# A two-layer decoder trunk: the products of the gate and up pairs and of the down pairs issued in source order

## The chip, the core and the metric

The kernel runs on one core of a Trainium2 chip. The metric is the device time of one launch in microseconds (us). The time before is the median of three runs.

## What is computed

The reference is a trunk of two layers for one sequence of 256 tokens and a width of 2048, all in float32. A layer has a mixing half (attention heads and a gated recurrence that share one input and one output projection), a feed-forward half, and a gated embedding at its end. Each half is normed before and after it:

```python
for i in range(DEPTH):                      # DEPTH = 2
    h = rms_norm(x, pre_mix_gain[i])
    m = hybrid_mixer(h, positions, w_in[i], ..., w_out[i])
    x = x + rms_norm(m, post_mix_gain[i])
    h = rms_norm(x, pre_ffn_gain[i])
    f = (jax.nn.silu(h @ w_ffn_gate[i]) * (h @ w_ffn_up[i])) @ w_ffn_down[i]
    x = x + rms_norm(f, post_ffn_gain[i])
    gate = jax.nn.sigmoid(rms_norm(x, ple_gain[i]) @ w_ple_gate[i])
    x = x + (p[i] @ w_ple_proj[i]) * gate
```

The three matrices of the feed-forward half are 2048 x 5632 (gate, up) and 5632 x 2048 (down). The change lies in their multiplications.

## The kernel before

**Products.** Tokens stand on the 128 partitions in two tiles, t = 0 and 1. A weight is read in chunks of 256 x 512 (`fetch_w`, two halves k of 128 rows). Each chunk is split into a high part `wh`, a cast by ScalarE (line 305), and a low part `wl`, a subtraction by VectorE (line 315); the activations are split likewise into `xh` and `xl` (lines 203 and 204, into tiles named `ck`). A product of one half of a chunk with one token tile is then three matmuls of 128 x 128 by 128 x 512 into one PSUM bank: xh by wh (line 431), xl by wh (line 434) and xh by wl (line 435). A chunk with one token tile is thus six matmuls. `strip` (lines 330 to 333) multiplies one column strip of a weight in this way.

**Pairs.** `paired` multiplies two column strips together, wa into the banks e and a (token tiles 0 and 1), wb into the banks c and d, where d is the bank u again. For most chunks it does so plainly (`plain`): wa over all other chunks, then wb over them. For one pair of chunks (q and q + 1, and a half of q + 2 in the gate and up pairs) it takes seven block products in the place of eight: sums and differences of the activations' four blocks (`mix(1)` to `mix(4)`, tiles named `sum` or `nat`) meet sums and differences of the weights' chunks, which VectorE makes in place in the raw chunks (`sub`, line 447). The order in the source is this. `fast()` makes u (a bank of the tag `ms`), which ScalarE copies out (`saved(u)`, line 440), then c, which is copied too, then e, then a. `plain` then takes the first of the other chunks with wa into e and a, and behind it `second()` is called: it adds the product of `mix(2)` onto u, nine matmuls with `sum` operands in a gate and up pair, six with `nat` operands in a down pair, and copies u out again. In a gate and up pair, and in most down pairs, `plain` then goes on with the rest of wa, and `third()` follows it: `mix(4)` onto c, `mix(3)` onto u, a third copy of u. With `mixed_order` (the first down pair of a group of three) the last two chunks of the group are left until `third()` and the other chunks of wb have been done, since the group's last hidden strip is then still on its way.

**What runs over what.** In the feed-forward half of a layer the 5632 hidden columns are 11 strips of 512, n = 0 to 10. Strip 0 is done by `strip`, strips 1 to 10 each by a gate and up pair (`gated`). They are taken in groups of 2, 3, 3 and 3 (`FF_GROUPS`); with the first group one strip more is made ahead. After each group come its down products: the four output strips as two pairs, or, in the last group, one pair and two single strips. A layer has so 10 gate and up pairs and 7 down pairs. `paired` also does the two pairs of the output projection `w_out` and one pair of the gated embedding at the layer's end (with `after`). A finished hidden strip goes through VectorE and DRAM (`shuffled`: a store and four fetches, line 264, into `nat` tiles), and `split_shuffled` splits its token tiles a few chunks later (`later`, `tick`).

**What sets the order.** ScalarE, VectorE and TensorE each carry out their own instructions in order and wait for each other by semaphores. The source is recorded first, and a scheduler then decides in which order the instructions of each engine stand; it may put one ahead of another of the source where data allow it. `tc.high_priority` and `behind(name)` (place after the instruction last marked by that name; "pe" is the last product) are used here and there to steer it. The buffers of weights are `wps` (7 of `wh`, 7 of `wl`) and `wpr` (10 raw chunks): a cast into a `wh` buffer waits until TensorE has finished with what was in it. PSUM has four banks `acc` (c, e, a among them) and four banks `ms` (u).

## Time and profile before

| | |
|---|---|
| median of the runs | 2397.57 us |
| lowest and highest | 2392.6 and 2398.31 us |
| the profiled execution's own time | 2398.53 us |
| its span, first to last instruction | 2396.7 us |
| mean granted clock of TensorE | 0.995 |
| TensorE busy (PE) | 2365.4 us, 99% of the span |
| VectorE busy (DVE) | 1997.5 us, 83% |
| ScalarE busy (ACT) | 1401.3 us, 58% |
| DMA engines, bytes moved | 506.04 MB, 211 GB/s over the span |

The profile is of one execution. PE is TensorE's matmuls, PEld its weight loads, DVE VectorE, ACT ScalarE, SP the engine that issues most DMAs. A row of the timeline has the start in us, the length, the engine, the line of the kernel, the operation, the tile written and the tile read by the program's names, their shapes, and in square brackets how long the engine was idle before and what ended that. Matmuls overlap: one starts 0.23 us behind another in a dense stretch and is shown 0.39 long. In the list of waits a row has the waiting engine, tile and line, then what released it, and then the total in us, the number of times and the longest.

### The profile page before, as it was taken

The page shows a single profiled execution, that of the slowest core. Times are in us where ns is not written, and L with a number is a line of the kernel's source. Part 1 is how long each engine was busy: PE and PEld are TensorE (multiplying, and loading weights), DVE is VectorE, ACT ScalarE, POOL GpSimd, SP SyncE. Part 2 cuts the span into 40 slices and gives each one's busy share as a digit, 9 for nine tenths or more (in the row PEclk, how much of TensorE's full clock was granted, in tenths as well). Part 3 has the DMA queues.
Part 4 walks back from the last instruction along what each step waited for, and adds up shares of the span by engine and source line. Part 5 has one row for each costly group of instructions (what it writes and reads, how often), then busy time and mean ns, then how long its engine had stood idle before and what let it go on. Part 6 is the DMA issues. An engine that isn't in the chain of part 4 may idle for free. (4 is left out here: it accounts for less than half of the span.)

```text
span 2396.7 us, 31644 instructions
## 1 busy us (share of the span) xinstructions
PE 2365.4 (99%) x10951; PEld 1955.7 (82%) x10951; DVE 1997.5 (83%) x2647; ACT 1401.3 (58%) x2000; POOL 104.3 (4%) x213
## 2 busy tenths in 40 slices
PE   9999999999999999999999999999999999999999
PEld 7888887878878878878788888878787888788787
DVE  7687987999988889887867879789898989888785
ACT  6555466566555655656656554565566565565564
POOL 3100001000000000001010000010000000000010
PEclk9999999999999999999999999999999999999999
DMA  8666467666557665765776563675667575666753
GB/s 290 213 193 198 145 211 252 205 226 231 194 198 236 214 228 180 270 213 189 233 224 211 174 223 129 226 255 176 228 211 230 195 256 185 205 220 237 242 166 132
DMA packets 301665, 506.04 MB, mean 211 GB/s; under 512 B 23712, under 2 KB 69696, under 8 KB 301504
## 3 DMA queue, kind: packets, MB, share of 16 engines
q1 hardware_dynamic: 301200, 503.93, 63.5%
q8 instruction: 86, 1.41, 0.2%
q14 instruction: 75, 0.61, 0.1%
q10 hardware_dynamic: 240, 0.07, 0.0%
q0 software_dynamic: 64, 0.02, 0.0%
HBM read 474.57 MB, written 29.36 MB: 210 GB/s over the span
## 5 line engine op out<-in xcount | busy, mean ns | idle before, releaser
L305 ACT CAST wh<-wr 128x1024 fp32r<-128x1024 f32 x980 | 1012.1, 1052 | 794.9 <-DVE wr L447 215.4
L315 DVE TENSOR_TENSOR wl<-wr,wh 128x1024 fp32r<-128x1024 f32 x980 | 1169.2, 1220 | 252.8 <-ACT wh L305 233.7
L330 PE MATMUL acc<-wh,ck 128*128 128x512 f32 x1056 | 417.8, 396 | 0.8 <-ACT ck L203 0.8
L331 PE MATMUL acc<-wh,ck 128*128 128x512 f32 x1056 | 413.5, 392 | 0.0
L333 PE MATMUL acc<-wl,ck 128*128 128x512 f32 x1056 | 411.9, 391 | 0.8 <-DVE wl L315 0.8
L447 DVE TENSOR_TENSOR wr<-wr 128x1024 f32<-128x1024 f32 (+1 forms) x240 | 243.4, 1042 | 1.2
L333 PEld LDWEIGHTS acc<-wl,ck 128*128 128x128 f32 x1056 | 198.5, 188 | 42.9 <-DVE wl L315 1.7
L331 PEld LDWEIGHTS acc<-wh,ck 128*128 128x128 f32 x1056 | 199.0, 188 | 40.2 <-DVE ck L204 0.4
L330 PEld LDWEIGHTS acc<-wh,ck 128*128 128x128 f32 x1056 | 198.5, 188 | 40.7 <-ACT ck L203 1.0
L431 PE MATMUL acce<-wh,ck 128*128 128x512 f32 x468 | 183.1, 391 | 8.6 <-ACT ck L203 8.6
L434 PE MATMUL acce<-wh,ck 128*128 128x512 f32 x468 | 183.6, 392 | 3.3 <-DVE ck L204 3.3
L431 PE MATMUL acca<-wh,ck 128*128 128x512 f32 x468 | 182.2, 389 | 0.6 <-ACT nat L1285 0.6
L435 PE MATMUL acce<-wl,ck 128*128 128x512 f32 x468 | 182.2, 389 | 0.0
L435 PE MATMUL acca<-wl,ck 128*128 128x512 f32 x468 | 182.1, 389 | 0.0
L434 PE MATMUL acca<-wh,ck 128*128 128x512 f32 x468 | 182.1, 389 | 0.0
L435 PE MATMUL ms<-wl,ck 128*128 128x512 f32 x440 | 171.5, 390 | 4.0 <-DVE wl L315 4.0
L431 PE MATMUL ms<-wh,ck 128*128 128x512 f32 x440 | 172.5, 392 | 0.0
L434 PE MATMUL ms<-wh,ck 128*128 128x512 f32 x440 | 171.3, 389 | 0.0
L434 PE MATMUL accc<-wh,ck 128*128 128x512 f32 x368 | 143.2, 389 | 0.0
L435 PE MATMUL accc<-wl,ck 128*128 128x512 f32 x368 | 143.2, 389 | 0.0
L431 PE MATMUL accc<-wh,ck 128*128 128x512 f32 x368 | 143.2, 389 | 0.0
L431 PEld LDWEIGHTS acce<-wh,ck 128*128 128x128 f32 x468 | 87.8, 188 | 28.8 <-ACT ck L203 11.1
(285 smaller groups left out, 3252.1 us busy)
## 6 DMA issues: line engine op xcount, KB each, us to landing
wr<-in_w_in_dram SPq DMA_DIRECT2D x176, 512.0 KB, 4.7
wr<-in_w_ffn_gate_dram SPq DMA_DIRECT2D x176, 512.0 KB, 5.2
wr<-in_w_ffn_up_dram SPq DMA_DIRECT2D x176, 512.0 KB, 6.0
wr<-in_w_ffn_down_dram SPq DMA_DIRECT2D x176, 512.0 KB, 6.9
wr<-in_w_out_dram SPq DMA_DIRECT2D x64, 512.0 KB, 4.6
wr<-in_w_ple_gate_dram SPq DMA_DIRECT2D x64, 512.0 KB, 5.0
turn<-nat SPq DMA_DIRECT2D x86, 256.0 KB, 2.6
nat<-turn SPq DMA_DIRECT2D x344, 64.0 KB, 3.5
```

The lines of the kernel that those rows point to most:

```text
L305: marks["hi"] = S.copy(hi, raw)
L315: marks["lo"] = V.tensor_tensor(lo, raw, hi.bitcast(F32), op=ALU.subtract)
L330: T.matmul(ps[t], xh, hi[:, k], start=first, stop=False)
L331: T.matmul(ps[t], xl, hi[:, k], start=False, stop=False)
L333: marks[t, c] = marks["pe"] = T.matmul(ps[t], xh, lo[:, k], start=False, stop=last)
L431: T.matmul(ps, xh, hi[:, k], start=id(ps) not in opened, stop=False, skip_group_check=True)
L434: T.matmul(ps, xl, hi[:, k], start=False, stop=False, skip_group_check=True)
L435: marks["pe"] = T.matmul(ps, xh, lo[:, k], start=False, stop=k == ks[-1], skip_group_check=True)
L447: V.tensor_tensor(dst, p, q, op=ALU.subtract)
```

## The change

`paired` gets an argument `free`. Its body after `fast()` becomes an inner function `products`, and for every pair that is neither `free` nor has `after` that body is recorded in a manual schedule for TensorE: TensorE's instructions keep the order in which the source issues them. `fast()` is placed behind the product issued last before it. The two `w_out` pairs are passed `free=True`, so they and the pair of the gated embedding are recorded as before. The order of the other engines is still the scheduler's.

```diff
@@ -410,7 +410,7 @@
         return both
 
     def paired(lhs, sums, wa, wb, cols, done_a, done_b, nch=8, row0=0, skews=(0, 0),
-               after=None, mixed_order=False, half=None, q=0):
+               after=None, mixed_order=False, half=None, q=0, free=False):
 
         base = row0 // (2 * P)
         opened = {}
@@ -529,30 +529,37 @@
             if end:
                 end(1)
 
-        e, a, c, d, x1, x2, second, third = fast()
-
-        def end_a(t):
-            done_a(t, (e, a)[t], x1[t])
-
-        def end_b(t):
-            done_b(t, (c, d)[t], x2[t])
-        if mixed_order:
-            plain(wa, cols[0], (e, a), 0, None, cs=rest[:-2], then=second)
+
+        def products(pin):
+            with behind("pe") if pin else nullcontext():
+                e, a, c, d, x1, x2, second, third = fast()
+
+            def end_a(t):
+                done_a(t, (e, a)[t], x1[t])
+
+            def end_b(t):
+                done_b(t, (c, d)[t], x2[t])
+            if mixed_order:
+                plain(wa, cols[0], (e, a), 0, None, cs=rest[:-2], then=second)
+                third()
+                plain(wb, cols[1], (c, d), 0, None, cs=rest[:-2])
+                plain(wa, cols[0], (e, a), 0, end_a, cs=rest[-2:])
+                plain(wb, cols[1], (c, d), 0, end_b, cs=rest[-2:])
+                return
+            def then():
+                second()
+                if after:
+                    after[0]()
+            plain(wa, cols[0], (e, a), skews[0], lambda t: t or end_a(t), then=then)
             third()
-            plain(wb, cols[1], (c, d), 0, None, cs=rest[:-2])
-            plain(wa, cols[0], (e, a), 0, end_a, cs=rest[-2:])
-            plain(wb, cols[1], (c, d), 0, end_b, cs=rest[-2:])
-            return
-        def then():
-            second()
+            end_a(1)
             if after:
-                after[0]()
-        plain(wa, cols[0], (e, a), skews[0], lambda t: t or end_a(t), then=then)
-        third()
-        end_a(1)
-        if after:
-            after[1]()
-        plain(wb, cols[1], (c, d), skews[1], end_b)
+                after[1]()
+            plain(wb, cols[1], (c, d), skews[1], end_b)
+
+        pin = not (after or free)
+        with tc.manual_schedule(engines={T.engine}) if pin else nullcontext():
+            products(pin)
 
     def load_gain(g, col):
         b = np_.tile([P, W], F32, tag="gB", name="gB", bufs=2)
@@ -1174,7 +1181,7 @@
             return summed(done)
         for s in (0, 2):
             paired(mixT, lambda: sums, w_out[l], w_out[l], (s * W, s * W + W), merged(s),
-                   merged(s + 1), skews=(0, SKEW if s == 2 else 0))
+                   merged(s + 1), skews=(0, SKEW if s == 2 else 0), free=True)
 
 
         rx2 = lazy_rstd(ss, "ry")
```

The following rows show the order of instructions on an engine; behind the names stand the buffers' numbers, which for one and the same buffer are up to 2 higher after the change than before it at the first place, and up to 20 higher at the second.

First place: the first gate and up pair of layer 0 (strip 1) on TensorE, where the first plain chunk of wa ends. `acca` and `acce` are the banks a and e, `ms` is u, `ck` the activations and `sum` their mixed sums. Before:

```order
L435 MATMUL acca_4342<-wl_4368,ck_3061 128x512
L431 MATMUL acce_4326<-wh_4399,ck_3063 128x512
L434 MATMUL acce_4326<-wh_4399,ck_3064 128x512
L435 MATMUL acce_4326<-wl_4401,ck_3063 128x512
L431 MATMUL acce_4326<-wh_4399,ck_3063 128x512
L434 MATMUL acce_4326<-wh_4399,ck_3064 128x512
L435 MATMUL acce_4326<-wl_4401,ck_3063 128x512
L431 MATMUL acca_4342<-wh_4399,ck_3063 128x512
L434 MATMUL acca_4342<-wh_4399,ck_3064 128x512
L435 MATMUL acca_4342<-wl_4401,ck_3063 128x512
L431 MATMUL acca_4342<-wh_4399,ck_3063 128x512
L431 MATMUL ms_4284<-wh_4382,sum_4069 128x512
```

After:

```order
L435 MATMUL acca_4344<-wl_4370,ck_3061 128x512
L431 MATMUL ms_4286<-wh_4384,sum_4069 128x512
L434 MATMUL ms_4286<-wh_4384,sum_4070 128x512
L435 MATMUL ms_4286<-wl_4386,sum_4069 128x512
L431 MATMUL ms_4286<-wh_4384,sum_4069 128x512
L434 MATMUL ms_4286<-wh_4384,sum_4070 128x512
L435 MATMUL ms_4286<-wl_4386,sum_4069 128x512
L431 MATMUL ms_4286<-wh_4357,sum_4085 128x512
L434 MATMUL ms_4286<-wh_4357,sum_4086 128x512
L435 MATMUL ms_4286<-wl_4359,sum_4085 128x512
L431 MATMUL acce_4328<-wh_4401,ck_3063 128x512
L434 MATMUL acce_4328<-wh_4401,ck_3064 128x512
```

The nine `ms` products of `second()` stood behind ten products of the second plain chunk (`wh_4399`); they now stand ahead of all of that chunk (`wh_4401` after). The product of the first chunk ahead of them is the same in both.

ScalarE at the same place, before; the copies are `saved(u)` and the copy of c, and L203 splits a hidden strip:

```order
L305 CAST wh_4457<-wr_4455 128x1024
L203 CAST ck_3822<-nat_4249 128x4x128
L305 CAST wh_4476<-wr_4282 128x1024
L440 COPY nat_4302<-ms_4284 128x512
L440 COPY nat_4324<-accc_4305 128x512
```

After:

```order
L305 CAST wh_4459<-wr_4457 128x1024
L203 CAST ck_3822<-nat_4249 128x4x128
L305 CAST wh_4478<-wr_4284 128x1024
L440 COPY nat_4304<-ms_4286 128x512
L440 COPY nat_4326<-accc_4307 128x512
```

Nothing has moved: the copy of `ms`, which `second()` needs, stands behind the same split and the same cast.

Second place: the first down pair of the second group of layer 0 (`mixed_order`) on TensorE. `wh_6118` and `wh_6150` before are the group's first plain chunks, and `ck_5687` and `ck_5688` the high and low part of its last hidden strip. Before:

```order
L435 MATMUL acca_6102<-wl_6120,ck_4623 128x512
L431 MATMUL acce_6089<-wh_6150,ck_4623 128x512
L434 MATMUL acce_6089<-wh_6150,ck_4624 128x512
...
L434 MATMUL acca_6102<-wh_6150,ck_4624 128x512
L435 MATMUL acca_6102<-wl_6152,ck_4623 128x512
L431 MATMUL acce_6089<-wh_6226,ck_5687 128x512
L434 MATMUL acce_6089<-wh_6226,ck_5688 128x512
L431 MATMUL ms_6062<-wh_6134,nat_5925 128x512
L434 MATMUL ms_6062<-wh_6134,nat_5927 128x512
L435 MATMUL ms_6062<-wl_6136,nat_5925 128x512
```

After:

```order
L434 MATMUL acca_6122<-wh_6138,ck_4627 128x512
L435 MATMUL acca_6122<-wl_6140,ck_4626 128x512
L431 MATMUL ms_6082<-wh_6154,nat_5942 128x512
L434 MATMUL ms_6082<-wh_6154,nat_5944 128x512
L435 MATMUL ms_6082<-wl_6156,nat_5942 128x512
...
L435 MATMUL ms_6082<-wl_6156,nat_5942 128x512
L431 MATMUL acce_6109<-wh_6170,ck_4626 128x512
L434 MATMUL acce_6109<-wh_6170,ck_4627 128x512
```

`second()` stood behind the second plain chunk and behind two products with the last hidden strip; now it stands between the first and the second plain chunk, and the products with the last strip come after `third()`.

ScalarE there, before:

```order
L305 CAST wh_6208<-wr_6206 128x1024
L305 CAST wh_6226<-wr_6224 128x1024
L305 CAST wh_6244<-wr_6242 128x1024
L203 CAST ck_5687<-nat_6032 128x4x128
L440 COPY nat_6073<-ms_6062 128x512
L440 COPY nat_6087<-accc_6076 128x512
L305 CAST wh_6266<-wr_6264 128x1024
L440 COPY nat_6144<-ms_6062 128x512
L305 CAST wh_6284<-wr_6282 128x1024
```

After:

```order
L305 CAST wh_6228<-wr_6226 128x1024
L305 CAST wh_6246<-wr_6244 128x1024
L203 CAST ck_5702<-nat_6049 128x4x128
L440 COPY nat_6093<-ms_6082 128x512
L440 COPY nat_6107<-accc_6096 128x512
L305 CAST wh_6264<-wr_6262 128x1024
L440 COPY nat_6164<-ms_6082 128x512
L203 CAST ck_5702<-nat_6066 128x4x128
L305 CAST wh_6286<-wr_6284 128x1024
```

The cast of `wh_6244` (now `wh_6264`) has moved behind the split of the last hidden strip and behind the first two copies; the copy of u still stands directly behind that split. The split of the strip's second half has moved ahead of one cast.

## The prediction

> **What bounds the kernel now.** I read the page first, then the waits of TensorE alone, then the timelines of TensorE and ScalarE around the places where the rows of TensorE move.

> ```profile
> span 2396.7 us, 31644 instructions
> PE 2365.4 (99%) x10951; PEld 1955.7 (82%) x10951; DVE 1997.5 (83%) x2647; ACT 1401.3 (58%) x2000; POOL 104.3 (4%) x213
> ```

> TensorE is busy through 99% of the span, so the time is its products, which the change neither adds to nor takes from, and the few places where it stands still. The waits of TensorE (us in total, times, longest):

> ```profile
> PE acce L431 <- ACT ck L203: 8.6, 6, 1.4
> PE ms L435 <- DVE wl L315: 4.0, 2, 2.0
> PE acce L434 <- DVE ck L204: 3.3, 6, 0.5
> ...
> PE accu L431 <- ACT nat L440: 1.2, 1, 1.2
> ```

> The first three lie in down pairs: the scheduler put products of a later step ahead, and their operands were not there. The fourth, in the last pair of the layer, shows a wait of another kind: `second()` adds onto the bank u, so it may not start before ScalarE has copied u out (line 440, `saved(u)`). In the gate and up pairs TensorE waits nowhere. So each change of order is to be asked two things: which of these waits goes, and is the copy of u done where `second()` now stands?

> **The gate and up pairs.** At the first moved one `second()` (ms<-wh,sum) moves ahead of ten products of the next chunk. The timeline of TensorE, then of ScalarE (start, length; idle before and what ended it in brackets):

> ```profile
> 449.35 0.39 PE L434 MATMUL acca<-wh,ck 128*128 128x512 f32 x1
> ...
> 449.80 0.39 PE L431 MATMUL acce<-wh,ck 128*128 128x512 f32 x1
> ...
> 452.07 0.39 PE L431 MATMUL ms<-wh,sum 128*128 128x512 f32 x1
> ```

> ```profile
> 448.37 0.62 ACT L203 CAST ck<-nat 128x512 fp32r<-128x512 f32 x1 [0.94 <-DMA nat<-turn]
> 449.78 1.06 ACT L305 CAST wh<-wr 128x1024 fp32r<-128x1024 f32 x1 [0.78 <-PE acca L434]
> 450.74 0.57 ACT L440 COPY nat<-ms 128x512 f32<-128x512 f32 x1
> ```

> Ten products take 452.07 - 449.80 = 2.27 us, 0.227 each. In the new order `second()` is due at 449.80. The copy that it needs runs from 450.74 to 451.31, because on ScalarE it stands behind the cast of a weight chunk, and that cast starts at 449.78, when the product of 449.35 has released its buffer. Both the cast and the copy hold their places in the new order, and the product that releases the buffer still stands ahead of `second()`. So nothing makes the copy earlier. The ten products, which covered it, are now behind it.

> How long TensorE takes after such a copy is seen in the layer's last pair:

> ```profile
> 1163.09 0.39 PE L330 MATMUL ms<-wh,pT 128*128 128x512 f32 x1
> 1164.64 0.50 PE L431 MATMUL accu<-wh,sum 128*128 128x512 f32 x1 [1.16 <-ACT nat L440]
> 1164.97 0.40 PE L434 MATMUL accu<-wh,sum 128*128 128x512 f32 x1
> ```

> ```profile
> 1164.02 0.56 ACT L440 COPY nat<-accu 128x512 f32<-128x512 f32 x1
> ```

> The copy ended at 1164.58 and the product started 0.06 later; the product behind it came 0.33 after it, 0.10 more than usual. (The idle time shown, 1.16, is less than the loss, 1.55 - 0.23 = 1.32, since the product before is counted for 0.39.) So here: 451.31 + 0.06 - 449.80 = 1.57, and with 0.10 a loss of 1.67 us. Thirteen pairs stand alike; the last of them is

> ```profile
> 2189.88 0.39 PE L431 MATMUL acce<-wh,ck 128*128 128x512 f32 x1
> ```

> ```profile
> 2190.80 0.58 ACT L440 COPY nat<-ms 128x512 f32<-128x512 f32 x1
> ```

> with 2191.38 + 0.06 - 2189.88 = 1.56. A fourteenth, the second pair of layer 1, has its copy later still:

> ```profile
> 1680.55 0.39 PE L431 MATMUL acce<-wh,ck 128*128 128x512 f32 x1
> ```

> ```profile
> 1682.46 0.57 ACT L440 COPY nat<-ms 128x512 f32<-128x512 f32 x1
> ```

> That is 1683.09 - 1680.55 = 2.54, or 2.64 with the 0.10. Together 13 x 1.67 + 2.64 = **24.3 us**. All of it is on the path, since TensorE stood still nowhere here, and what comes later (casts, splits, the transposes of the hidden strip) hangs on TensorE's own progress and moves with it. Of the other six gate and up pairs, the first behind a group's down pairs, four keep their rows and two change in one place each that waits for no copy: nothing. The weights that `second()` multiplies are no limit; the scheduler had them made in the order of the source.

> **The first down pair of a layer (2 places).** A product of the next pair was put ahead and waited for its low weights:

> ```profile
> 530.04 0.39 PE L431 MATMUL acce<-wh,ck 128*128 128x512 f32 x1
> ...
> 532.99 0.39 PE L434 MATMUL ms<-wh,ck 128*128 128x512 f32 x1
> 535.40 0.50 PE L435 MATMUL ms<-wl,ck 128*128 128x512 f32 x1 [2.02 <-DVE wl L315]
> ```

> ```profile
> 532.07 0.57 ACT L440 COPY nat<-ms 128x512 f32<-128x512 f32 x1
> ```

> This wait goes: 2.41 - 0.23 + 0.11 = 2.29 us. But `second()` is now due at 530.04 and its copy ends at 532.64, so it loses 2.66 + 0.10. Net **+0.8 us** for the two.

> **The other down pairs that open a group (6 places).** Here two products of the group's last hidden strip stood ahead of `second()` and waited for that strip's split:

> ```profile
> 656.45 0.39 PE L431 MATMUL acce<-wh,ck 128*128 128x512 f32 x1
> ...
> 658.94 0.39 PE L435 MATMUL acca<-wl,ck 128*128 128x512 f32 x1
> 660.76 0.50 PE L431 MATMUL acce<-wh,ck 128*128 128x512 f32 x1 [1.43 <-ACT ck L203]
> 661.81 0.51 PE L434 MATMUL acce<-wh,ck 128*128 128x512 f32 x1 [0.55 <-DVE ck L204]
> 662.15 0.40 PE L431 MATMUL ms<-wh,nat 128*128 128x512 f32 x1
> ```

> ```profile
> 656.42 1.06 ACT L305 CAST wh<-wr 128x1024 fp32r<-128x1024 f32 x1 [1.66 <-PE acca L434]
> ...
> 660.10 0.61 ACT L203 CAST ck<-nat 128x512 fp32r<-128x512 f32 x1
> 660.62 0.58 ACT L440 COPY nat<-ms 128x512 f32<-128x512 f32 x1
> ```

> These go: 1.59 + 0.82 + 0.11 = 2.52 each, 15.1 in all. In the new order `second()` is due at 656.45, and its copy stands behind that same split on ScalarE, which now follows the cast of 656.42 directly. The split waits for four DMAs, and so does the next one, of the strip's other half:

> ```profile
> L264 SPq DMA_DIRECT2D nat<-turn x4: 327/422/432, 653.4 to 654.7; - x4
> DMA to landing us min/median/max: 3.1/3.4/3.6
> ```

> ```profile
> L264 SPq DMA_DIRECT2D nat<-turn x4: 328/422/430, 659.1 to 660.4; - x4
> DMA to landing us min/median/max: 3.8/4.3/4.4
> ```

> The first four have landed at 654.7 + 3.1 = 657.8. Split at 657.9, copy 0.52 later (660.62 - 660.10), 0.58 long, 0.06: TensorE starts at 659.06, a loss of 2.61 + 0.10 = 2.71, 16.3 in all. A third copy follows: `third()` leaves u to be copied again before the next ms product, 36 products behind the start of `second()`, at 659.06 + 0.10 + 8.17 = 667.3. On ScalarE this copy stands behind the second split, whose DMAs land at 660.4 + 3.8 = 664.2, and three casts (two in a layer's last group): 664.3 + 0.5 + 3 x 0.96 + 0.6 = 668.3. So up to 1.0 us more where three casts stand, at least nothing; the estimate is 0.7 for each of the six, 4 in all. Sum: 16.3 - 15.1 + 4 = **+5 us**.

> **The clock of TensorE.** Windows of the trace; each row has the window, its length, the busy time and instructions of PE, PEld, DVE, ACT and POOL, the granted clock, the busy DMA share and GB/s. First a pair from two places:

> ```profile
> 848.30:851.70 3.40, 1.43 (x6) 0.61 (x5) 3.40 (x5) 2.54 (x4) 0.00 (x0) 1.00 0.93 295
> 1848.40:1851.80 3.40, 1.97 (x10) 1.31 (x8) 3.40 (x4) 1.74 (x4) 0.00 (x0) 1.00 0.81 262
> ```

> Then what followed the first of them, and the last stretch of this kind:

> ```profile
> 851.70:855.10 3.40, 3.40 (x8) 2.72 (x9) 1.04 (x1) 0.48 (x1) 0.00 (x0) 0.50 1.01 252
> ...
> 2234.10:2237.40 3.30, 3.30 (x8) 2.62 (x9) 0.97 (x1) 0.50 (x1) 0.00 (x0) 0.50 0.94 330
> ```

> The stretch from 848.30 has 3.40 - 1.43 = 1.97 us without TensorE, and 3.4 us at half clock (0.50) followed: 8 products where 15 fit at 0.227, 1.6 us lost. The stretch from 1848.40 has 1.43 idle, and none followed. There are five such halvings at the eight down pairs (first and last shown), 8.0 us. The new waits of 1.57 show as 1.57 - 0.16 = 1.41 idle: just under, none counted. The nine long ones (eight down pairs, the fourteenth pair) show 2.4 or so. Cut by a grid of 3.4 us, 2.4 leaves under 1.7 on both sides in (2 x 1.7 - 2.4)/3.4 = 0.3 of the cases; so 6 to 7 of 9 halve, 10.4 us, **+2.4**.

> [...]

> **Sum:** 24.3 + 0.8 + 5 + 2.4 = 32.5 us on the profiled execution's 2398.5 (span 2396.7 and 1.8 around it): 2431. The median of the runs shown is 1 us less, so I forecast **2430 us**, 1.4% slower.

> **The rivals.**
> - *Faster.* The waits at the eight down pairs go and nothing takes their place: 2 x 2.29 + 15.1 + 8.0 = 27.7 less, 2371. It needs the copies of u 1.6 us earlier (2.6 at the down pairs), ended by 449.80 at the first; from there the change gains. For it: the product that is copied was finished long before. Against it: the copy's place on ScalarE, behind a cast that TensorE itself releases. 0.05.
> - *Absorbed.* The lateness is made up at waits that shrink. Against it: those waits hang on TensorE's own progress. Also here, that the order on the chip is not what the rows show. About 2398. 0.05.
> - *Half clock at the short waits too.* If 1.41 us is enough, a wait falls whole into one stretch in 1 - 1.41/3.4 = 0.59 of thirteen: 12.3 more, 2443. Against it: the 1.43 above. 0.09.
> - [...] 0.07.
> - The forecast: 0.74.

> **Range.** Below: no loss at third copies (-4) and no halvings (-10.4) give 2416, and 2 us for the runs' own spread; above, the half-clock rival's 2443: 2414 to 2443. A measurement of this kernel tells about 0.3% (7 us) from no change. Slower by more: 0.90 (the forecast and the two clock rivals); within it: 0.05; faster: 0.05.

> **What would show it.** Among TensorE's waits, acce from L203 and ms from L435 on wl should be gone, and a new row of ms L431 from ACT nat L440 should stand with about 22 waits, fourteen with sum operands near 1.4 (one 2.4) and eight with nat near 2.4. I am wrong if that row is absent, if the copies start before `second()` is due, or if the lost time lies in other pairs than these.

## The result

The changed kernel takes 2432.05 us (median of four runs, 2426.37 to 2435.57); before it took 2397.84 (four runs, 2392.6 to 2398.31). The ratio is 1.0145, with a 95% interval of 1.0121 to 1.017: 34 us slower. The forecast was 2430, the range 2414 to 2443. The profiled execution took 2433.15 us. Its page begins:

```profile
span 2431.0 us, 31669 instructions
...
PE 2369.8 (97%) x10951; PEld 1955.9 (80%) x10951; DVE 2003.2 (82%) x2647; ACT 1403.2 (58%) x2000; POOL 105.6 (4%) x213
```

TensorE has the same 10951 matmuls and is busy for 4 us more, while the span is 34 us longer: the time is in places where it stands still. The waits of TensorE after the change (us in total, times, longest) say for what:

```profile
PE ms L431 <- ACT nat L440: 45.9, 26, 2.7
...
PE accu L431 <- ACT nat L440: 1.1, 1, 1.1
```

The first row is new. The three rows that led the list before (acce from L203, ms from wl, acce from L204; 15.9 us together) are gone. The first moved pair, on TensorE and then on ScalarE (start, length; idle before and what ended it):

```profile
447.99 0.39 PE L435 MATMUL acca<-wl,ck 128*128 128x512 f32 x1
449.77 0.50 PE L431 MATMUL ms<-wh,sum 128*128 128x512 f32 x1 [1.39 <-ACT nat L440]
450.11 0.40 PE L434 MATMUL ms<-wh,sum 128*128 128x512 f32 x1
```

```profile
446.85 0.62 ACT L203 CAST ck<-nat 128x512 fp32r<-128x512 f32 x1 [1.00 <-DMA nat<-turn]
448.19 1.04 ACT L305 CAST wh<-wr 128x1024 fp32r<-128x1024 f32 x1 [0.71 <-PE acca L434]
449.14 0.58 ACT L440 COPY nat<-ms 128x512 f32<-128x512 f32 x1
```

All of it comes about 1.6 us earlier than before, because this execution left out the half clock with which the one before began (granted clock 0.50 from 8.58 to 11.99 us); the rest is as it was. The cast waits for the product that frees its buffer, the copy ends at 449.72, `second()` starts at 449.77. It was due at 447.99 + 0.23 = 448.22, so it starts 1.55 late, and the next product comes 0.34 behind it and not 0.23.

**Where the 34 us are.** The two traces have the same number of matmuls, and outside the moved stretches the same one at the same place in the row. So the start of a matmul after, less that of the same one before, taken on both sides of each pair, gives what the pair lost:

| part | forecast | measured |
|---|---|---|
| fourteen gate and up pairs | 24.3 | 24.9: eleven of 1.69, the others 2.34, 1.98, 2.03 |
| the other six gate and up pairs | 0 | -0.2 |
| eight down pairs, clock included | 0.8 + 5 + 2.4 = 8.2 | 11.3: -0.6 to 3.3 each |
| second down pairs of the first groups | 0 | -0.3 |
| the rest, the clock at the start above all | 0 | -1.3 |
| sum | 32.5 | 34.4 |

In a down pair that opens a later group, TensorE and ScalarE now show this:

```profile
661.59 0.39 PE L435 MATMUL acca<-wl,ck 128*128 128x512 f32 x1
664.68 0.79 PE L431 MATMUL ms<-wh,nat 128*128 128x512 f32 x1 [2.71 <-ACT nat L440]
```

```profile
661.78 1.04 ACT L305 CAST wh<-wr 128x1024 fp32r<-128x1024 f32 x1 [1.66 <-PE acca L434]
663.52 0.62 ACT L203 CAST ck<-nat 128x512 fp32r<-128x512 f32 x1 [0.69 <-DMA nat<-turn]
664.04 0.58 ACT L440 COPY nat<-ms 128x512 f32<-128x512 f32 x1
```

The split stands directly behind that cast and waits for its DMA, and the copy stands behind the split. The eight waits of this kind are 2.36 to 2.71 us long.

### The profile page after: what moved, and what is told of

Same layout as the page of the kernel before. It is cut to its first block, busy times and chain, and to the rows that moved or that the text cites. A ratio compares the mean times of both kernels' runs of the same rounds, so it can differ in the third digit from the quotient of the medians.

```text
span 2431.0 us, 31669 instructions
## 1 busy us (share of the span) xinstructions
PE 2369.8 (97%) x10951; PEld 1955.9 (80%) x10951; DVE 2003.2 (82%) x2647; ACT 1403.2 (58%) x2000; POOL 105.6 (4%) x213
## 3 DMA queue, kind: packets, MB, share of 16 engines
q8 instruction: 86, 1.41, 0.2%
## 4 chain that ended last, share of the span: by engine, by line
PE 85%; DVE 5%; DMA 4%; issue 2%; ACT 2%; SPq 1%; POOL 1%; ACTq 0%; DVEq 0%; POOLq 0%
PE acc L331 9%; PE acc L330 9%; PE acc L333 9%; PE ms L431 5%; PE ms L434 5%; PE ms L435 5%; PE accc L435 5%; PE accc L434 5%; PE accc L431 5%; PE acce L431 4%; PE acce L434 4%; PE acce L435 4%; PE acca L434 4%; PE acca L431 4%; PE acca L435 4%; DMA nat<-turn 2%
## 5 line engine op out<-in xcount | busy, mean ns | idle before, releaser
L305 ACT CAST wh<-wr 128x1024 fp32r<-128x1024 f32 x980 | 1012.4, 1052 | 815.2 <-PE acca L434 219.1
L315 DVE TENSOR_TENSOR wl<-wr,wh 128x1024 fp32r<-128x1024 f32 x980 | 1171.1, 1219 | 275.5 <-ACT wh L305 264.5
L330 PE MATMUL acc<-wh,ck 128*128 128x512 f32 x1056 | 417.1, 395 | 0.7 <-ACT ck L203 0.7
L330 PEld LDWEIGHTS acc<-wh,ck 128*128 128x128 f32 x1056 | 198.2, 188 | 40.5 <-ACT ck L203 0.9
L431 PE MATMUL acce<-wh,ck 128*128 128x512 f32 x468 | 184.1, 393 | 0.0
L434 PE MATMUL acce<-wh,ck 128*128 128x512 f32 x468 | 183.2, 391 | 0.0
L431 PE MATMUL acca<-wh,ck 128*128 128x512 f32 x468 | 182.5, 390 | 0.7 <-ACT nat L1292 0.7
L435 PE MATMUL acce<-wl,ck 128*128 128x512 f32 x468 | 182.9, 391 | 0.0
L434 PE MATMUL acca<-wh,ck 128*128 128x512 f32 x468 | 182.3, 390 | 0.0
L435 PE MATMUL acca<-wl,ck 128*128 128x512 f32 x468 | 182.1, 389 | 0.0
L431 PE MATMUL ms<-wh,ck 128*128 128x512 f32 x440 | 172.6, 392 | 4.8 <-ACT nat L440 4.6
L435 PE MATMUL ms<-wl,ck 128*128 128x512 f32 x440 | 171.6, 390 | 0.0
L434 PE MATMUL ms<-wh,ck 128*128 128x512 f32 x440 | 171.3, 389 | 0.0
L431 PE MATMUL accc<-wh,ck 128*128 128x512 f32 x368 | 143.7, 390 | 0.0
L435 PE MATMUL accc<-wl,ck 128*128 128x512 f32 x368 | 143.6, 390 | 0.0
L434 PE MATMUL accc<-wh,ck 128*128 128x512 f32 x368 | 143.6, 390 | 0.0
L431 PEld LDWEIGHTS acce<-wh,ck 128*128 128x128 f32 x468 | 88.8, 190 | 18.6
```

Of the source, the lines that this page charges most:

```text
L305: marks["hi"] = S.copy(hi, raw)
L315: marks["lo"] = V.tensor_tensor(lo, raw, hi.bitcast(F32), op=ALU.subtract)
L330: T.matmul(ps[t], xh, hi[:, k], start=first, stop=False)
L431: T.matmul(ps, xh, hi[:, k], start=id(ps) not in opened, stop=False, skip_group_check=True)
L434: T.matmul(ps, xl, hi[:, k], start=False, stop=False, skip_group_check=True)
L435: marks["pe"] = T.matmul(ps, xh, lo[:, k], start=False, stop=k == ks[-1], skip_group_check=True)
```

## The experiments

Each kernel differs from the changed one (after) by the edit shown; of the last three, it is shown against the run with all copies early. Dots stand between places of the kernel that lie apart. The first four ran together on one chip with the kernel before, then the next three, then the last two; the ratios are to the runs of before beside them.

| run | us | ratio | 95% interval |
|---|---|---|---|
| only the gate and up pairs in source order | 2425.06 | 1.0118 | 1.0103 to 1.0133 |
| only the down pairs in source order | 2407.37 | 1.0043 | 1.0028 to 1.0058 |
| after, copy of u ahead of the casts in the gate and up pairs | 2410.32 | 1.0053 | 1.0036 to 1.0069 |
| after, first copy of u made twice | 2463.71 | 1.0278 | 1.0263 to 1.0294 |
| after, `second()` a chunk later in the gate and up pairs | 2405.96 | 1.0038 | 1.0026 to 1.005 |
| after, all these copies early | 2390.38 | 0.9972 | 0.9962 to 0.9983 |
| the same, nothing in source order | 2387.84 | 0.9959 | 0.9946 to 0.9971 |
| early copies but for the first down pairs, in source order | 2384.76 | 0.9946 | 0.9932 to 0.996 |
| the same, nothing in source order | 2382.88 | 0.9941 | 0.9928 to 0.9953 |

Theory A is the prediction's: `second()` now comes before the copy of u is made. Theory B is that the order as such costs the time: a free scheduler keeps TensorE ahead with products that are ready, a fixed order does not, whatever it then waits for.

### Which pairs

```diff
-                           mixed_order=s == 1 and glen > 2, q=2)
+                           mixed_order=s == 1 and glen > 2, q=2, free=True)
```

> Only the gate and up pairs are issued in source order; the down pairs are free as before. Theory A (the copy of u is late for second(), and nothing else): the fourteen waits of ms on the copy, with sum operands, stand as after, the six waits of acce on the split and the two of ms on wl in the down pairs stand as before; 2398 + 24.8 = about 2423 us, 2419 to 2427. Theory B (pinning spoils the order as a whole, and the loss comes from the two kinds of pairs together): not near 2423; under 2410, or all of 2432.

Measured: 2425.06, inside theory A's span. The waits of TensorE in this run:

```profile
PE ms L431 <- ACT nat L440: 19.9, 14, 1.7
PE acce L431 <- ACT ck L203: 8.6, 6, 1.4
PE ms L435 <- DVE wl L315: 4.0, 2, 2.0
PE acce L434 <- DVE ck L204: 3.3, 6, 0.5
```

Fourteen new ones, and the three rows of before to the digit. The other half:

```diff
             paired(xT, lambda: sx[0], w_ffn_gate[l], w_ffn_up[l], (col, col), summed(done_gate),
-                   summed(done_up), half=lambda: sx[1])
+                   summed(done_up), half=lambda: sx[1], free=True)
```

> Only the down pairs are issued in source order; the gate and up pairs are free. Theory A: no wait with sum operands, eight waits of ms on the copy of u with nat operands of 2.4 to 2.7 us and some on the third copy, no wait on the split or on wl; 2398 + 10.8 (what the down pairs lost in the trace of after) = about 2409 us, 2404 to 2413, so that the two parts add up to the 34 of both. Theory B: the parts do not add up.

Measured: 2407.37. The waits:

```profile
PE ms L431 <- ACT nat L440: 20.8, 10, 2.7
```

Eight long ones and two short ones on later copies; the rows on the split and on wl are gone. The two parts are 28 and 10 us against the runs before beside them, 38 where both together gave 34, and their intervals (3.6 us either way for each) cover the difference. Matmul by matmul against before, the two traces end 26.6 and 7.9 us late, 34.4 together; of the 26.6, 3.1 lie in down pairs that wait as before, behind which the clock fell to half at two places more than before. So the loss is a sum over pairs.

### The copy, moved on ScalarE alone

TensorE's rows are exactly those of after. In the gate and up pairs one cast is placed behind the copy:

```diff
-            x = [saved(u)]
+            b = nat()
+            marks["u"] = S.copy(b, u)
+            x = [b]
...
-                    ws[i] = load_w(w, base + cs[i], col)
+                    raw = fetch_w(w, base + cs[i], col)
+                    with behind("u") if half and then and i == 1 else nullcontext():
+                        hi = high(raw)
+                    ws[i] = load_w(w, base + cs[i], col, raw, hi)
```

> As after, with TensorE's rows unchanged; in the gate and up pairs ScalarE's cast of the second plain chunk is placed behind the copy of u, so that the copy stands ahead of five casts. Theory A: the copy then hangs on the split's DMA alone (448.4 + 0.6 + 0.6 in the first pair) and is there at about 449.5, ahead of the 449.8 at which second() is due; the fourteen waits shrink from 1.4 to under 0.3 us, two or three that have a late split keep up to 1 us; 2432 - 24.8 + 2 = about 2409 us, 2405 to 2414. Theory B (the order of TensorE's products itself costs the time, since nothing covers the weights' casts any more): TensorE's order is that of after, so 2432 or more, with new waits on the casts and on wl.

Measured: 2410.32, where theory B gives 2432 or more. TensorE and ScalarE at the first pair:

```profile
448.32 0.39 PE L435 MATMUL acca<-wl,ck 128*128 128x512 f32 x1
448.55 0.43 PE L431 MATMUL ms<-wh,sum 128*128 128x512 f32 x1
```

```profile
447.32 0.62 ACT L203 CAST ck<-nat 128x512 fp32r<-128x512 f32 x1 [5.17 <-DMA nat<-turn]
447.85 0.58 ACT L468 COPY nat<-ms 128x512 f32<-128x512 f32 x1
...
448.80 2.01 ACT L305 CAST wh<-wr 128x1024 fp32r<-128x1024 f32 x2
```

`second()` follows its predecessor by 0.23, without a stop. ScalarE is idle for 5.17 us ahead of the split, which waits for its DMA, and still the copy is in time, since it no longer stands behind the cast. Two of the fourteen waits are left, 1.68 and 1.21 us long. With TensorE's order the same, the order of ScalarE alone took away about 20 of the 24.9 us: this is what decides between A and B.

### The copy, made later

```diff
             x = [saved(u)]
+            S.copy(x[0], u)
```

> As after, but the first copy of u is made twice, into the same place; the second stands behind the copy of c, so u is free about 1.0 us later (two copies by the spacing of 0.5 us). Theory A: each of the 22 waits grows by 1.0 us, 22 us; the short ones are then 2.4 us long and some of the thirteen halve the clock (up to 9 of them by 1.6 us): 2454 to 2470, likeliest 2464. Theory B (the copy is not what TensorE waits for): 20 us more work for ScalarE, which is busy 58%, so 2432 to 2435.

Measured: 2463.71, on the forecast of theory A. The waits of TensorE, its row at the first pair, and ScalarE's:

```profile
PE ms L431 <- ACT nat L468: 63.4, 22, 3.9
```

```profile
451.11 0.80 PE L431 MATMUL ms<-wh,sum 128*128 128x512 f32 x1 [2.37 <-ACT nat L468]
```

```profile
449.50 0.58 ACT L440 COPY nat<-ms 128x512 f32<-128x512 f32 x1
449.98 0.59 ACT L440 COPY nat<-accc 128x512 f32<-128x512 f32 x1
450.45 0.60 ACT L468 COPY nat<-ms 128x512 f32<-128x512 f32 x1
```

The second copy ends 0.97 later than the first, and the short waits grew by 0.98, from 1.39 to 2.37. The number of waits is 22, as expected. Fewer of the fourteen waits with sum operands halved the clock than expected (5, expected up to 9). The waits at third copies, 4.6 us after the change, are absent here; the forecast did not have that, so that the total falls on it is in part luck.

### More products ahead of second()

```diff
-                if then and i == 0:
+                if then and i == (1 if half else 0):
```

> As after, but in the gate and up pairs the source calls second() behind the second plain chunk and not behind the first; all is still issued in source order, and ScalarE's order around the copy is that of after. Theory A: twelve products, 2.7 us, now cover the copy, which needs 1.6 (2.5 in one place): the fourteen waits go, and the loss of the down pairs stays: 2432 - 24.8 = about 2407 us, 2404 to 2412. Theory B: issued in source order as after, so about 2432.

Measured: 2405.96. TensorE at the first pair, where `second()` would have been due at 453.62 - 12 x 0.227 = 450.90 in the order of after, and ScalarE's copy:

```profile
453.40 0.39 PE L435 MATMUL acca<-wl,ck 128*128 128x512 f32 x1
453.62 0.39 PE L431 MATMUL ms<-wh,sum 128*128 128x512 f32 x1
```

```profile
451.84 0.58 ACT L440 COPY nat<-ms 128x512 f32<-128x512 f32 x1
```

The copy ends at 452.42, and the product that needs it starts 1.20 later, without a stop. Here everything is still issued in source order and the copy was not made earlier; all fourteen pairs lost nothing. So it isn't pinning that costs, but pinning to a source in which one chunk stands between a's products and `second()`.

### All copies early

This is the test of the rival that had the kernel faster (2371): what if no copy of u is late? To the edit of ScalarE's order above, now in every pair (those of `w_out` and of the gated embedding too), come

```diff
-            split(d, h, lo)
+            with behind("u", "hi"):
+                split(d, h, lo)
...
-                x.append(saved(u))
+                b = nat()
+                marks["u"] = S.copy(b, u)
+                x.append(b)
...
-            wait = 3 if last else 6
+            wait = 5 if last else 6
```

and the cast of the first of the two late chunks is placed behind the third copy.

> TensorE's rows are those of after. On ScalarE, in all these pairs, the cast of the second plain chunk stands behind the first copy of u; where the last two chunks come late, the cast of the first of them stands behind the third copy; the split of a hidden strip is recorded two ticks later in a group's last strip and stands behind the latest copy and cast. So no copy of u stands behind a DMA or a cast that TensorE releases. Theory A: all waits of ms on a copy go, 24.8 us in the gate and up pairs, and the down pairs give what the rival 'faster' of the prediction counted: 2398 less 2.3 x 2, 2.5 x 6 and five halvings of 1.6, about 2370 us; the casts of the second chunk, now later, may cost a few us: 2368 to 2380. Theory B (TensorE's order itself is what costs): TensorE's order is that of after, so 2432 or more.

Measured: 2390.38. Theory B fails, since in all pairs of the change TensorE has the rows of after (19 products of the gated embedding's pair, which was never in source order, stand otherwise); but so does theory A's figure of 2370. No product waits for a copy of u any more. The waits that are there:

```profile
PE acca L432 <- ACT wh L306: 5.7, 6, 2.3
PE acca L436 <- DVE wl L316: 4.5, 7, 0.9
```

```profile
546.26 0.40 PE L436 MATMUL acce<-wl,ck 128*128 128x512 f32 x1
548.99 0.79 PE L432 MATMUL acca<-wh,ck 128*128 128x512 f32 x1 [2.33 <-ACT wh L306]
```

The pairing of matmuls with before gives -0.2 us in the gate and up pairs, -21.0 in the six later down pairs, but +4.9 and +2.4 at the first down pairs of the layers and +1.4 in the gate and up pair behind each: weights of the next pair (549) come late there. Four of the second down pairs (of each layer's second and third group) lose 1.2 to 1.4 each, 5.3 in all, to the same two waits: 0.26 us idle for a cast and 0.53 for low weights. The same edits with nothing in source order:

```diff
-        pin = not (after or free)
+        pin = False
```

> The same edits of ScalarE's order, but no pair is issued in source order. The scheduler then puts second() at its place in the source by itself in the gate and up pairs. Theory A: what counts is when the copies are made and not the pinning, so within 5 us of the run with the same copies and pinned order: 2368 to 2382. Theory B': the pinning is worth something by itself once the copies are early (no product ahead whose low weights or split are missing): 10 us or more slower than that run.

Measured: 2387.84, 2.5 us from the run above: as theory A has it, the pinning is worth little either way once the copies are early. The expected 2368 to 2382 is missed for the same reason as above.

### The copies early, except in the first down pairs

```diff
-                    with behind("u") if (1 if then else late) == i else nullcontext():
+                    with behind("u") if (half or mixed_order) and (1 if then else late) == i else nullcontext():
...
-            wait = 5 if last else 6
+            wait = (5 if n > 2 else 3) if last else 6
...
-                           mixed_order=s == 1 and glen > 2, q=2)
+                           mixed_order=s == 1 and glen > 2, q=2, free=gi == 0)
```

The strips up to n = 2 also lose the `behind` of their splits. The first condition does more than the heading says: in the second down pairs, in the pairs of `w_out` and in that of the gated embedding the cast is back at its old place too.

> As the run with all copies first, but the first down pairs of a layer, their hidden strip and ScalarE's order in them are as before, and free. Theory A: what that run lost there (4.9 and 1.8 us in layer 0, 2.4 and 1.4 in layer 1, by waits on casts that came late) is back, 10.5 us: 2390.4 - 10.5 = about 2380 us, 2377 to 2384. If the waits on casts were a matter of ScalarE's work as a whole and not of this place: 2390 as there.

Measured: 2384.76, with a ratio of 0.9946 to before; half of the expected step, and just past the end of the span. The waits of this run:

```profile
PE ms L436 <- DVE wl L316: 4.0, 2, 2.0
PE acca L436 <- DVE wl L316: 2.1, 4, 0.5
PE acca L432 <- ACT wh L306: 1.1, 4, 0.3
PE ms L432 <- ACT nat L469: 0.8, 2, 0.5
```

The wait on wl in the first down pairs is back, as before, 2.0 us each. By the pairing, the first down pairs stand at +1.5 and -1.5 against before: the half clock behind that wait fell in the other layer. So what the run with all copies early lost at this place, 9.7 us with the pairs behind, is back but for 0.4. The step is smaller for other reasons. Three gate and up pairs lost 0.5 to 0.9 us each; in two of them, as the last row shows, the copy of u was late again. Why it is late in those and not there was not tried. The embedding's pair of layer 0, where the cast is back, waits for its copy again (0.8 us) and is 1.9 us worse than there. The second and the third row are the waits of the four second down pairs above, which still lose about 1.4 us each.

And the same with `pin = False`:

> The same edits, nothing issued in source order. Theory A: within 3 us of the run with the same copies and pinned order, about 2380 us, 2375 to 2385; if issuing in source order has a price or a gain of its own when the copies are early, more than 5 us apart.

Measured: 2382.88, 1.9 us from the pinned one, as expected. These two are faster than before and after; the gain lies in ScalarE's order, not in TensorE's.

## Why the prediction was right, step by step

- **The gate and up pairs.** Right in kind, place and size: fourteen waits, 1.67 expected and 1.69 found in eleven. The fourteenth pair, with a late split, had 2.03 where 2.64 was forecast, and two others were later than they stood before. In one of them the split's DMA came late:

```profile
816.71 0.62 ACT L203 CAST ck<-nat 128x512 fp32r<-128x512 f32 x1 [1.89 <-DMA nat<-turn]
817.24 1.04 ACT L305 CAST wh<-wr 128x1024 fp32r<-128x1024 f32 x1
818.18 0.58 ACT L440 COPY nat<-ms 128x512 f32<-128x512 f32 x1
```

  The prediction took it that what hangs on TensorE moves with it. That holds for the cast, and not quite for the DMA. The sum, 24.9, is 0.6 off. Two of the six pairs that were to cost nothing gained 0.1 each.
- **Nothing is made up later.** Right: from the last moved pair of layer 0 to the first of layer 1, over 575 us, the distance to before changes by 0.2 us.
- **The first down pairs.** The waits on wl went, and `second()` starts 2.8 and 2.5 late where 2.66 was forecast. By the prediction's own terms the net is 2 x (2.76 - 2.29) = 0.9 and not 0.8. Measured are 2.2 and -0.6: the one half clock behind these pairs fell in layer 1 before and in layer 0 after.
- **The later down pairs.** The waits on the split went, all six, and the copies came 2.5 to 2.9 late (2.61 forecast). The third copies cost 4.6 us of waits in four of the six places where 4 in all was forecast, but most unevenly: 0.2, 2.7, 1.3 and 0.5. The largest:

```profile
871.46 0.50 PE L431 MATMUL ms<-wh,ck 128*128 128x512 f32 x1 [2.73 <-ACT nat L440]
```

```profile
867.46 0.62 ACT L203 CAST ck<-nat 128x512 fp32r<-128x512 f32 x1 [4.19 <-DMA nat<-turn]
867.99 2.94 ACT L305 CAST wh<-wr 128x1024 fp32r<-128x1024 f32 x3
870.83 0.57 ACT L440 COPY nat<-ms 128x512 f32<-128x512 f32 x1
```

  It is the chain that was forecast: second split, three casts, copy. The bound of "up to 1.0 us" was too tight: the split's DMA landed later than taken (ScalarE idle for 4.19). All eight down pairs together cost 11.3 where 8.2 was forecast, the largest miss of the sum. Later copies (about 0.6), third copies (0.6) and the clock (0.8) make up 2.0 of these 3.1; the rest is not assigned.
- **The clock.** Forecast: 6 to 7 of the nine long waits halve it, none of the short ones. Found: six stretches of half clock, one of them twice as long, five at down pairs' `second()` and one at a third copy; none at the short waits. So five of the nine long waits halved it and not 6 to 7; the third copy's stretch and the doubled one, which the prediction did not have, bring the windows at half clock to seven. That the term comes out near (11.2 for 10.4) is luck. Windows of the trace (PE, PEld, DVE, ACT and POOL busy, the granted clock, the DMA share and GB/s), a long wait and a short one, each with the window behind it:

```profile
661.01:664.42 3.41, 0.96 (x5) 0.46 (x3) 3.41 (x4) 1.94 (x3) 0.00 (x0) 1.00 0.98 245
664.42:667.83 3.41, 3.15 (x7) 2.48 (x8) 2.69 (x3) 1.31 (x3) 0.00 (x0) 0.50 1.00 284
490.34:493.75 3.41, 2.02 (x10) 1.34 (x9) 3.41 (x5) 2.02 (x3) 0.00 (x0) 1.00 1.02 312
493.75:497.16 3.41, 3.41 (x17) 2.81 (x16) 2.35 (x3) 2.76 (x4) 0.00 (x0) 1.00 1.04 276
```

  2.45 us of idle in a window halved the clock, 1.39 did not. The rival of half clock at short waits (2443) falls, and so does a time without any halving, the 10.4 us less of the range. The 1.7 us by which the prediction counted the halvings was its author's estimate, midway between the 1.43 and the 1.97 of its rows; no run shows it as an edge. In the runs 1.84 and 1.90 us idle halved the clock, 1.69 and 1.88 did not.
- **The total.** It is 2 us from the forecast, and closer than its terms: the 3.7 more in the moved pairs are in part made up by the half clock at the start, which this execution did not have (1.6), and by 0.5 in pairs that were to cost nothing.
- **The rival "faster".** It needed the copies 1.6 us earlier (2.6 in the down pairs). With the copies that early the kernel is faster, but by 7 to 16 us and not by 27: in their place came waits on casts and on low weights, which the sum of 2371 did not price.

## What to carry to other kernels

An order that a scheduler chose may look wrong against the source and still be cover for something slow on another engine; before undoing it, look up at which time the operand of the moved instruction is ready, and by which engine's queue. An engine that is busy 58% can be the one that sets the time, if the one short instruction that matters stands behind another that waits for the busy engine or for a DMA. The cure is then in the order of that engine, and in these runs moving one cast per pair (2432.05 to 2410.32 us) gave more than fixing the order of thousands of products.

## What the runs showed of the hardware

The length of a wait alone does not tell it. After the change the wait of 2.71 us that ends at 664.68 put 2.45 us idle into one window and halved the clock. The wait of 2.54 us that ends at 1058.40 lies across two windows (from 1053.54 and from 1056.95, TensorE busy for 2.32 of 3.41 and 1.97 of 3.42), with 1.09 and 1.45 us idle, and full clock followed behind both. Two windows of the run with the copy made twice, each with the one behind it:

```profile
1850.33:1853.74 3.41, 1.53 (x7) 0.94 (x5) 3.41 (x5) 2.71 (x6) 0.00 (x0) 1.00 0.99 331
1853.74:1857.15 3.41, 2.92 (x13) 2.43 (x14) 1.59 (x3) 1.89 (x4) 0.00 (x0) 1.00 0.98 299
1720.62:1724.03 3.41, 1.51 (x7) 1.25 (x8) 2.44 (x3) 1.89 (x5) 0.00 (x0) 1.00 0.67 186
1724.03:1727.44 3.41, 3.41 (x10) 2.65 (x9) 1.61 (x2) 2.94 (x4) 0.00 (x0) 0.50 1.06 385
```

1.88 us idle did not halve it, 1.90 did. But the edge is not that sharp: before the change a window with 1.84 us idle (from 1039.41, TensorE busy for 1.57 of 3.41) halved it. What else decides between 1.84 and 1.90 is open. Behind a window that itself ran at half clock, half clock followed once in the traces of before and after, with 0.68 us idle (from 1872.74 after the change), and full clock eleven times, with 0 to 0.26 us idle; why so little was enough there is open.
